# A seven-product form for the third row pair of a decoder's gate and up projection

## The chip, the core and the metric

The kernel runs on one NeuronCore of a Trainium2 chip. The engines named below are TensorE (PE, matrix products; PEld is its loading of the stationary operand), VectorE (DVE), ScalarE (ACT), GpSimd (POOL) and SyncE (SP, which issues most DMAs). They run side by side, each through its own queue of instructions, and wait for one another through semaphores. The metric is the device time of one execution in microseconds, the median of several runs.

## The reference

Two pre-norm residual layers over 256 tokens of width 2048, in float32. Each has a token mixer (HGRN2 in the first, gated linear attention in the second) beside a cross-attention into 256 memory tokens, an output projection, and a SwiGLU feed-forward of inner width 5632. The change lies in the last of these:

```python
hn = _rmsnorm(h, norm_ffn[layer])
gate, up = jnp.split(hn @ w_gate_up[layer], 2, axis=-1)
h = h + (jax.nn.silu(gate) * up) @ w_down[layer]
```

Here `hn` is 256 x 2048 and `w_gate_up[layer]` is 2048 x 11264.

## The kernel before

**Two halves of each number.** Float32 operands are split in two parts of the format fp32r: a high part (a cast on ScalarE) and a low part (the operand minus the high part, on VectorE; once in a block on GpSimd). One product of a 128x128 left block with a 128x512 right block then takes three matmuls: high x high, high x low, low x high. The function `split` (line 276) makes the two parts of a loaded weight tile `raw`; the names `parts148a` to `parts148d` in the trace are those of tile number 148.

**Row pairs.** The 2048 rows of the weight are eight pairs of 256 rows. For one pair and one block of 512 columns of gate and 512 of up, the work is a product of 2 x 2 blocks: two token tiles by two row tiles on the left, two row tiles by two column groups on the right. A plain product has eight block products. A pair of kind **S** does with seven, in Winograd's manner: `seven` (line 420) first splits the weight blocks b00, b11 and b10, then makes three differences and sums on VectorE in place (`raw<-raw`: one of 128x1024, two of 128x512), and splits the results t5, t7, t6, t4. A pair of kind **O** uses eight products and needs no arithmetic on the weights, only on the left factors (`d0`, `d1`). A pair of kind **H** uses eight products too, with one weight difference: one subtraction of 128x512 on VectorE, then the split of the result `e1`. The left factors of each pair are made once a layer by `Forms` (line 359); which there are depends on the pair's letter in `PAIRS` (line 354): six for O (with `d1`, without `s`, `u`, `z`), eight for S, nine for B. A pair whose factors are those of S can be used as S or as H; one with `d1` as O.

**Blocks.** `ffn` (line 1172) runs over 11 blocks of 512 inner columns. `up_block(b)` calls `project_halves` (line 591) with a string of eight letters from `KINDS` (line 1161), one for each pair; blocks from number 4 on use the last string. PE's products of a block accumulate in seven PSUM banks, named `f_p` in the trace. For S the order of the seven products of a pair is 1, 3, 2, 5, 7, 6, 4, and in the block's last pair 1, 2, 6, 7, 5, 4, 3. Then VectorE sums the banks to gate and up (`sums`, the tiles `e` and `s`), ScalarE and VectorE form silu(gate) x up (`gate`), PE transposes the result (`turn`), and two pieces of the down projection of an earlier block follow on PE (`fd` in the trace), each with a copy of `h` into its bank and a give-back to `h` by ScalarE (`h<-fd`).

**Order.** With `Engine.kept` set (line 608, from pair 3 of block 0 on and through all further blocks) the instructions keep the order in which the program names them, on every engine. Small pieces (`sums`, `gate`, `turn`, the give-backs) are put in by keys: `due` files a piece, and `mark` issues all that are due, at places inside the preparation of weights. So what ScalarE and VectorE do between two weight parts is written out by hand.

**Buffers.** `raw` has three buffers. The parts of two row groups (tag `parts`) have six; the parts of a single row group of 512 columns (tag `part`: part a of S, part c of H) have two. A buffer is used again when its readers, matmuls of PE, are done.

The tile numbers in the trace run on: block 0 of layer 0 has 84 to 91, block 1 has 92 to 99, then come tiles of the down projection; block 2 has 102 to 109, block 3 has 112 to 119, block 4 has 124 to 131, block 5 has 136 to 143, block 6 has 148 to 155. Hereafter a pair is named by its place in the block, 0 to 7, or by its tile's number.

Of the kernel before, what the change touches and what calls it, by code (L numbers as in the profile page):

```python
# [26 lines left out]
DFF = 5632  # L27
# [13 lines left out]
def trunk_kernel(ctx: ExitStack, tc: tile.TileContext, x, mem, norm_mix, norm_ffn, norm_mem,  # L41
# [12 lines left out]
    def bank(name):  # L54
        return psum.tile([P, 512], F32, tag="bank", name=name)
# [84 lines left out]
    class Engine:  # L140
        kept = False

        def __init__(self, engine):
            self.engine = engine
            self.last = self.hold = None
# [33 lines left out]
    def mark(key):  # L179
        while waiting and waiting[0][0] <= key:  # L180
            waiting.pop(0)[2]()
# [14 lines left out]
    class Quad:  # L196
# [6 lines left out]
        def x(self, k, t):  # L203
            return self.h[:, k, t * P:(t + 1) * P], self.l[:, k, t * P:(t + 1) * P]
# [13 lines left out]
    def transposes(srcs, name, back=False):  # L218

        ps = aux_ps(name)  # L220
        turns(ps, [src(t) for src in srcs for t in range(NT)], (ident, turned_id if back else ident))
        return ps
# [29 lines left out]
    def later(*pieces):  # L252
        pending.extend(pieces)

    def step():
        if pending:
            piece = pending.pop(0)
            if piece:
                piece()
# [11 lines left out]
    def new_raw():  # L271
        i = n_w[0]
        n_w[0] += 1
        return i, wts.tile([P, 4, 512], F32, tag="raw", name=f"raw{i}", bufs=3)
# [76 lines left out]

    PAIRS = "SSOSSOSB"
    HOMES = (("hq", "hq"),) * 4 + (("F", "K"), ("T", "sc"), ("Q", None), ("v", "gate"))
    FACTORS = {"S": ("x10", "x00", "x01", "x11", "s", "d0", "u", "z"), "O": ("x10", "x00", "x01", "x11", "d0", "d1"),
               "B": ("x10", "x00", "x01", "x11", "s", "d0", "u", "z", "d1")}
# [1 line left out]
    class Forms:  # L359


        def __init__(self, p, name):
            self.kind = PAIRS[p]
            self.names = FACTORS[self.kind]
# [43 lines left out]
    def load_pair(raw, w, p, c0, c1, n):  # L408

        if n_w[0] == 1:  # L410
            for k, j, c in ((0, 0, c0), (0, 1, c1), (1, 3, c0), (1, 2, c1)):
                nc.sync.dma_start(out=raw[:, j, 0:n], in_=w[(2 * p + k) * P:(2 * p + k + 1) * P, c:c + n])
                if k == 0 and c == c1:
                    load_mem(0, 256, 512)
            return
        for j, c in ((slice(0, 4, 3), c0), (slice(1, 3), c1)):
            nc.sync.dma_start(out=raw[:, j, 0:n],
                              in_=w[2 * p * P:(2 * p + 2) * P, c:c + n].rearrange("(k p) c -> p k c", p=P))

    def seven(i, raw, between=None):  # L420

        n = raw.shape[2]
        tt = ve.tensor_tensor
        b00, = split(raw[:, 0:1, :], f"{i}a")
        b11, b10 = split(raw[:, 2:4, :], f"{i}b")
        if between:
            between()

        tt(out=raw[:, 0:2, :], in0=raw[:, 0:4:2, :], in1=raw[:, 1:2, :].broadcast_to([P, 2, n]), op=ALU.subtract)
        tt(out=raw[:, 2, :], in0=raw[:, 2, :], in1=raw[:, 0, :], op=ALU.add)  # L430
        tt(out=raw[:, 3, :], in0=raw[:, 3, :], in1=raw[:, 2, :], op=ALU.subtract)
        t5, t7 = split(raw[:, 0:2, :], f"{i}c")
        t6, t4 = split(raw[:, 2:4, :], f"{i}d")
        return {1: ("x00", b00), 2: ("x01", b10), 3: ("z", b11), 4: ("x11", t4), 5: ("s", t5), 6: ("u", t6), 7: ("d0", t7)}
# [81 lines left out]
    def project_two(pairs, plan, w, c0, c1, n, name, give, view=lambda ps: ps, onto=None, prep=None, behind=None,  # L516
# [10 lines left out]
        else:  # L527
            sevens, plains = iter(range(len(PAIRS))), iter(range(plan.count("S"), len(PAIRS)))
            order = [next(sevens if c == "S" else plains) for c in plan]
# [61 lines left out]
    def project_halves(forms, kinds, w, c0, c1, name, key, keep):  # L591


        left = {b: sum(TIMES[kind][b - 1] for kind in kinds) for b in range(1, 8)}
        ps = {}

        def product(b, left_factor, right):
            first = b not in ps
            if first:
                ps[b] = bank(f"{name}p{b}")  # L600
            left[b] -= 1
            (xh, xl), (hi, lo) = left_factor, right
            pe.matmul(ps[b], xh, hi, start=first, stop=False)
            pe.matmul(ps[b], xh, lo, start=False, stop=False)
            pe.matmul(ps[b], xl, hi, start=False, stop=left[b] == 0)

        for p, kind in enumerate(kinds):
            Engine.kept = keep <= p
            i, raw = new_raw()
            load_pair(raw, w, p, c0, c1, 512)  # L610
            x = forms[p].get
            last = p == len(PAIRS) - 1
            if kind == "S":
                todo = seven(i, raw, lambda: mark(key + p))
                for b in (1, 2, 6, 7, 5, 4, 3) if last else (1, 3, 2, 5, 7, 6, 4):
                    product(b, x(todo[b][0]), todo[b][1])
            else:
                b00, b01 = split(raw[:, 0:2, :], f"{i}a")
                mark(key + p)
                b11, b10 = split(raw[:, 2:4, :], f"{i}b")  # L620
                todo = [[(2, "x00", b00), (5, "x10", b01), (4, "x10", b00), (3, "d0", b01)]]
                if kind == "O":
                    todo.append([(2, "x01", b10), (5, "x11", b11), (4, "x11", b10), (3, "d1", b11)])
                else:
                    ve.tensor_tensor(out=raw[:, 3, :], in0=raw[:, 3, :], in1=raw[:, 2, :], op=ALU.subtract)
                    e1, = split(raw[:, 3:4, :], f"{i}c")
                    todo.append([(2, "x01", b10), (3, "x01", b11), (7, "x11", b11), (4, "x11", e1)])
                todo = [m for ms in zip(*todo) for m in ms] if last else todo[0] + todo[1]
                for b, f, right in todo:
                    product(b, x(f), right)  # L630
            step()
        return ps
# [56 lines left out]
    def more_of(quads, p, tag, name, behind=None):  # L689
        pairs = quads["pairs"]  # L690
        pairs[p] = held(behind, More, quads[p // 2], p % 2, tag, name) if behind else More(quads[p // 2], p % 2, tag, name)

    def quad_pairs(quads):
        quads["pairs"] = {p: Half(quads, p) for p in range(len(PAIRS))}

# [44 lines left out]
    for l in range(2):  # L740
# [6 lines left out]
        if l == 0:  # L747
            later(*[lambda p=p: more_of(memq, p, "hq", f"mem{p}") for p in range(len(PAIRS))
                    if f"{p}S" in MEM[1] and f"{p}S" not in MEM[0]])
# [408 lines left out]
    PARTS = ((0,), (1, 2), (3, 4), (5, 6), (7, 8), (9, 10))  # L1158


    KINDS = ("SHOSHOSO", "HHOSSOSO", "SHOSSOSO", "SSOSSOHS", "SSOSSOSS")

# [7 lines left out]
    def ffn(l, forms, r, after, tail=None):  # L1172
        sq = {}

        def up_block(b):
            ps = project_halves(forms, KINDS[min(b, 4)], w_gate_up[l], 512 * b, DFF + 512 * b, f"f{l}_{b}_",
                                100 * b, 0 if b else 3)
            when = WHEN[min(b, 3)]
            got = {}

            def sums():
                got["e"] = e = work.tile([P, NT, 512], F32, tag="stg", name=f"e{l}_{b}", bufs=2)
                got["s"] = s = work.tile([P, NT, 512], F32, tag="stg", name=f"s{l}_{b}", bufs=2)
                e0, e1, s0, s1 = e[:, 0, :], e[:, 1, :], s[:, 0, :], s[:, 1, :]
                ac.copy(out=e0, in_=ps[1])
                for out, p, q in ((s0, 2, e0), (e1, 6, e0), (s1, 7, e1), (e1, 5, e1), (e0, 5, s1),
                                  (s1, 4, s1), (e1, 3, e1)):
                    ve.tensor_tensor(out=out, in0=ps[p], in1=q, op=ALU.add)
                    if p == 2 and b:
                        free_port.append(ve.last)  # L1190

            def gate():
                e, s = got["e"], got["s"]
                for t in range(NT):
                    ac.activation(out=s[:, t, :], in_=s[:, t, :], func=AF.Silu, scale=r[:, t:t + 1])
                for t in range(NT):
                    ve.scalar_tensor_tensor(out=s[:, t, :], in0=e[:, 1 - t, :], scalar=r[:, t:t + 1], in1=s[:, t, :],
                                            op0=ALU.mult, op1=ALU.mult)

            def turn(j):  # L1200
                if j == 0:
                    sq[b] = Quad("tq", f"s{l}_{b}")
                got[j] = transposes([lambda t, c=(2 * j + i) * P: got["s"][:, t, c:c + P] for i in range(2)],
                                    f"tp_{sq[b].h.name}{j}")

            due(100 * b + when["sums"], sums)
            due(100 * b + when["gate"], gate)
            for j, (k0, k1) in enumerate(when["turn"]):
                due(100 * b + k0, lambda j=j: turn(j))
                due(100 * b + k1, lambda j=j: sq[b].put(2 * j, 2, got[j]))  # L1210
# [178 lines left out]
```

## Time and profile before

| | |
|---|---|
| median of 3 runs | 2271.93 us (2270.59 to 2271.93) |
| the profiled execution, its own time | 2271.69 us |
| its span, first to last instruction | 2269.9 us |
| TensorE clock granted, mean | 0.999 |
| feed-forward of layer 0, blocks 0 to 10, first product to the end of the last `f_p` | 524.2 to 1149.9 us |
| the same of layer 1 | 1572.0 to 2197.9 us |

A block from number 4 on takes 62.30 us in both layers, with one exception of 62.56.

How to read the rows shown below. A timeline row has the start in us from the span's begin, the duration in us, the engine, the line, the operation, what it writes and reads, and in brackets the idle time of the engine before it with what ended that time. Most rows have line 151, that of a helper that records the order, so the tiles' names tell what an instruction is. Where an engine starts an instruction before the end of the one ahead, the step from start to start is what counts. A row of stretches has the length, then busy time (and count) of PE, PEld, DVE, ACT and POOL, the granted clock, the share of the DMA engines and GB/s. One word on blocks: the tile numbers 136 to 143 and the stretch from 838 to 900 us do not belong to the same block; in that stretch PE works on the down projection behind block 5 and then on block 6 (148 to 155).

### The profile page before, as it was taken

Reading aid. Unit: us, or ns where it says so; the run is one execution under the profiler, and the core shown is the slowest. Engines: PE = TensorE matmul, PEld = TensorE weight load, DVE = VectorE, ACT = ScalarE, POOL = GpSimd, SP = SyncE. Lnnn points to the kernel's source line nnn. Section 1 sums busy time; section 2 is a strip of 40 time slices with the busy share of each in tenths; the row PEclk is TensorE's granted clock in tenths of the full one; section 3 lists DMA queues with packets and bytes.
Section 4 is the critical chain, followed back from the end, with each engine's and each line's share of the span. In section 5 each row is a group of like instructions: output and inputs, shape, how many; then the busy total and the mean of one; then the engine's idle time right before and its main releaser. Section 6 shows DMA issues by size and latency. Waiting matters only on the chain.

```text
span 2269.9 us, 29374 instructions
## 1 busy us (share of the span) xinstructions
PE 2250.8 (99%) x10710; PEld 1901.4 (84%) x10710; DVE 2065.8 (91%) x2615; ACT 1423.5 (63%) x1938; POOL 83.4 (4%) x61
## 2 busy tenths in 40 slices
PE   9999999999999999999999999999999999999998
PEld 7888888888888888888889999988888888888887
DVE  7889999899999999999996887899899999999997
ACT  6655656566666666666665665566566666666664
POOL 0000000000000000000000000001000000000000
PEclk9999999999999999999999999999999999999999
DMA  8645545455556665555665446555556565665564
GB/s 289 204 151 183 186 157 177 167 168 203 170 202 222 204 206 190 203 199 204 204 212 174 142 146 190 157 176 203 197 194 203 205 210 194 205 205 202 205 217 153
DMA packets 232644, 435.78 MB, mean 192 GB/s; under 512 B 13199, under 2 KB 42675, under 8 KB 232243
## 3 DMA queue, kind: packets, MB, share of 16 engines
q1 hardware_dynamic: 231203, 429.64, 56.4%
q10 hardware_dynamic: 1296, 4.26, 0.5%
q8 instruction: 84, 1.38, 0.2%
q14 instruction: 61, 0.50, 0.1%
HBM read 430.71 MB, written 3.15 MB: 191 GB/s over the span
## 4 chain that ended last, share of the span: by engine, by line
PE 89%; DVE 6%; ACT 2%; issue 1%; DMA 1%; POOL 0%; SPq 0%; POOLq 0%; DVEq 0%; ACTq 0%
PE f_p L151 39%; PE fd L151 19%; PE wo L151 4%; PE m1p L151 2%; PE wo0p L151 2%; PE hf0p L151 2%; PE wo1p L151 2%; PE fd_0p L151 2%; PE gk1p L151 1%; PE gg11p L151 1%; PE gg10p L151 1%; PE gg01p L151 1%; PE m0p L151 1%; DVE raw L151 1%; PE gx L151 1%
## 5 line engine op out<-in xcount | busy, mean ns | idle before, releaser
L151 DVE TENSOR_TENSOR raw<-raw 128x512 f32<-128x512 f32 (+3 forms) x474 | 403.6, 852 | 9.2
L151 ACT CAST parts<-raw 128x1024 fp32r<-128x1024 f32 (+1 forms) x216 | 212.0, 1016 | 44.6 <-DMA raw<-in_w_down_dram 9.8
L151 DVE TENSOR_TENSOR parts<-raw,parts 128x1024 fp32r<-128x1024 f32 (+1 forms) x196 | 224.0, 1180 | 15.2 <-ACT parts L151 15.1
L286 POOL TENSOR_TENSOR parts<-raw,parts 128x1024 fp32r<-128x1024 f32 x20 | 48.2, 2411 | 1187.1 <-ACT parts L151 1138.6
L151 ACT COPY h<-fd 128x512 f32<-128x512 f32 x80 | 46.3, 588 | 55.0 <-PE fd L151 52.1
L151 ACT ACTIVATE s<-s,rf_r 128x512 f32<-128x512 f32 x44 | 31.8, 722 | 41.6 <-DVE s L151 41.4
L151 DVE TENSOR_TENSOR e<-f_p,e 128x512 f32<-128x512 f32 x66 | 45.2, 685 | 2.3
L151 ACT COPY fd<-h 128x512 f32<-128x512 f32 x82 | 45.2, 582 | 0.0
L151 PE MATMUL fd<-parts,s_6h 128*128 128x512 f32 x128 | 39.8, 392 | 0.0
L151 PE MATMUL fd<-parts,s_8h 128*128 128x512 f32 x128 | 39.8, 392 | 0.0
L151 PE MATMUL fd<-parts,s_4h 128*128 128x512 f32 x128 | 39.8, 392 | 0.0
L151 PE MATMUL fd<-parts,s_2h 128*128 128x512 f32 x128 | 39.8, 392 | 0.0
L151 PE MATMUL fd<-parts,s_0h 128*128 128x512 f32 x128 | 39.8, 392 | 0.0
L151 PE MATMUL fd<-parts,s_5h 128*128 128x512 f32 x128 | 39.4, 389 | 0.0
L151 PE MATMUL fd<-parts,s_3h 128*128 128x512 f32 x128 | 39.4, 389 | 0.0
L151 PE MATMUL fd<-parts,s_7h 128*128 128x512 f32 x128 | 39.4, 389 | 0.0
L151 PE MATMUL fd<-parts,s_1h 128*128 128x512 f32 x128 | 39.4, 389 | 0.0
L151 DVE TENSOR_TENSOR s<-f_p,e 128x512 f32<-128x512 f32 x44 | 30.3, 689 | 4.3 <-PE f_p L151 2.4
L151 DVE SCALAR_TENSOR_TENSOR s<-e,rf_r,s 128x512 f32<-128x512 f32 x44 | 31.0, 747 | 0.2
L151 PEld LDWEIGHTS fd<-parts,s_7h 128*128 128x128 f32 x128 | 24.0, 188 | 5.0
L151 PEld LDWEIGHTS fd<-parts,s_3h 128*128 128x128 f32 x128 | 24.0, 188 | 5.0
L151 PEld LDWEIGHTS fd<-parts,s_1h 128*128 128x128 f32 x128 | 24.0, 188 | 5.0
(5723 smaller groups left out, 7258.1 us busy)
## 6 DMA issues: line engine op xcount, KB each, us to landing
raw<-in_w_gate_up_dram SPq DMA_DIRECT2D x352, 512.0 KB, 3.9
raw<-in_w_down_dram SPq DMA_DIRECT2D x80, 1024.0 KB, 5.7
raw<-in_hgrn_w_in_dram SPq DMA_DIRECT2D x96, 512.0 KB, 3.9
raw<-in_gla_w_in_dram SPq DMA_DIRECT2D x96, 384.0 KB, 3.3
raw<-in_w_out_dram SPq DMA_DIRECT2D x16, 1024.0 KB, 5.8
raw<-in_w_out_dram SPq DMA_DIRECT2D x32, 512.0 KB, 4.1
raw<-in_w_mem_kv_dram SPq DMA_DIRECT2D x30, 512.0 KB, 5.5
raw<-in_w_down_dram SPq DMA_DIRECT2D x16, 512.0 KB, 4.1
```

Source lines behind the costliest of these rows:

```text
L151: ins = func(*args, **kwargs)
L286: low = (nc.gpsimd if free_port else ve).tensor_tensor(out=both[:, 1, k:j, 0:m], in0=src[:, k:j, :], in1=both[:, 0, k:j, 0:m].bitcast(F32) ...
```

## The change

Pair 2 gets the eight left factors of kind S in place of the six of kind O. It can no longer be used as O, since `d1` is missing. So every string of `KINDS` changes in its third letter: in blocks 0 to 3 and in blocks 5, 7 and 9 from O to H, in blocks 4, 6, 8 and 10 from O to S. The same holds in both layers. All other letters stay.

```diff
-    PAIRS = "SSOSSOSB"
+    PAIRS = "SSSSSOSB"
...
-    KINDS = ("SHOSHOSO", "HHOSSOSO", "SHOSSOSO", "SSOSSOHS", "SSOSSOSS")
+    KINDS = ("SHHSHOSO", "HHHSSOSO", "SHHSSOSO", "SSHSSOHS") + ("SSSSSOSS", "SSHSSOSS") * 3 + ("SSSSSOSS",)
...
-            ps = project_halves(forms, KINDS[min(b, 4)], w_gate_up[l], 512 * b, DFF + 512 * b, f"f{l}_{b}_",
+            ps = project_halves(forms, KINDS[min(b, len(KINDS) - 1)], w_gate_up[l], 512 * b, DFF + 512 * b, f"f{l}_{b}_",
```

The number of products that each PSUM bank receives is counted from the string (`left` in `project_halves`, by `TIMES`, line 406), so it follows by itself. The loads of the weights do not change.

## The prediction

> **What bounds the kernel now.** I read the page first: the busy shares, then the chain that ended last.
>
> ```profile
> PE 2250.8 (99%) x10710; PEld 1901.4 (84%) x10710; DVE 2065.8 (91%) x2615; ACT 1423.5 (63%) x1938; POOL 83.4 (4%) x61
> ...
> PE 89%; DVE 6%; ACT 2%; issue 1%; DMA 1%; POOL 0%; SPq 0%; POOLq 0%; DVEq 0%; ACTq 0%
> ```
>
> TensorE looks like the only bound, and fewer matmuls look like the way to gain. But a busy share says nothing of how late the next operand comes, so I took one feed-forward period (block 6 of layer 0 with the down projection ahead of it) and cut it into stages: the time before VectorE's first work on the block's weights, the stretch in which VectorE prepares them, and the rest.
>
> ```profile
> 838.20:850.40 12.20, 12.20 (x55) 10.13 (x54) 10.36 (x13) 8.51 (x13) 2.28 (x1) 1.00 0.81 273
> 850.40:897.20 46.80, 46.80 (x212) 38.58 (x211) 45.71 (x49) 28.30 (x34) 0.00 (x0) 1.00 0.55 185
> 897.20:900.50 3.30, 3.30 (x15) 2.71 (x15) 3.30 (x4) 3.30 (x6) 0.14 (x1) 1.00 0.65 189
> sum 62.30, PE 62.30 PEld 51.42 DVE 59.37 ACT 40.11 POOL 2.42; mean PE 20.77 PEld 17.14 DVE 19.79 ACT 13.37 POOL 0.81
> ```
>
> (Columns: busy of PE, weight loads, DVE, ACT, POOL, then the granted clock.) PE is busy for all 62.30 us. DVE is idle for 2.93 us of the block (62.30 - 59.37), but 1.84 of these lie in the first stage; in the 46.80 us in which it prepares the eight row pairs it is busy for 45.71. So the question is which engine arrives last at the end of that stretch. The timeline of DVE, then of PE:
>
> ```profile
> 895.90 1.23 DVE L151 TENSOR_TENSOR parts155d<-raw,parts155d 128x1024 fp32r<-128x1024 f32 x1
> ```
>
> ```profile
> 896.89 0.78 PE L151 MATMUL f_p<-parts155d,hf_7h 128*128 128x512 f32 x2
> 897.51 0.39 PE L151 MATMUL f_p<-parts155d,hf_7l 128*128 128x512 f32 x1
> ...
> 899.82 0.62 PE L151 MATMUL f_p<-parts155b,hf_7h 128*128 128x512 f32 x2
> 900.27 0.39 PE L151 MATMUL f_p<-parts155b,hf_7l 128*128 128x512 f32 x1
> 900.50 0.62 PE L151 MATMUL fd<-parts,s_3h 128*128 128x512 f32 x2
> ```
>
> The last part of the last pair is done at 897.13 (895.90 + 1.23). The two matmuls that read it first take 0.78 where the same two take 0.62 at 899.82: PE waits 0.16 us for it, and everything behind runs without a gap to the down projection at 900.50, that is 3.37 us after DVE's end. **The up phase of every late block ends 3.37 us after DVE's last part; PE has no slack to give.** Nor can DVE begin sooner:
>
> ```profile
> 850.47 0.69 DVE L151 TENSOR_TENSOR parts148a<-raw,parts148a 128x512 fp32r<-128x512 f32 x1 [1.60 <-ACT parts148a L151]
> ```
>
> ```profile
> 848.66 1.27 ACT L151 COPY h<-fd 128x512 f32<-128x512 f32 x2 [1.78 <-PE fd L151]
> ```
>
> DVE idles 1.60 us before the block's first part, for ScalarE's cast of it; that cast stands in ACT's fixed order behind the give-back of `h`, which waits for the down projection on PE. The start of DVE's chain is thus tied to PE's last block, and its length from 850.47 to 897.13 sets the next end. That 45 us chain is what the change edits.
>
> **The change part by part.** *Matmuls removed.* A pair of kind S makes seven products, O and H eight, of three matmuls each. From 899.82 to 900.50 one product takes 0.68 us, 0.227 a matmul. Eight blocks (numbers 4, 6, 8, 10 in two layers) drop one: 8 x 0.68 = 5.4 us of PE. O to H removes none.
>
> *Pair 2 from O to S* in those eight. Block 6 holds an O (150) beside an S (151), in DVE's order:
>
> ```profile
> 865.50 1.22 DVE L151 TENSOR_TENSOR parts150a<-raw,parts150a 128x1024 fp32r<-128x1024 f32 x1
> 866.64 1.22 DVE L151 TENSOR_TENSOR parts150b<-raw,parts150b 128x1024 fp32r<-128x1024 f32 x1
> 867.77 0.69 DVE L151 TENSOR_TENSOR parts151a<-raw,parts151a 128x512 fp32r<-128x512 f32 x1
> 868.37 1.22 DVE L151 TENSOR_TENSOR parts151b<-raw,parts151b 128x1024 fp32r<-128x1024 f32 x1
> 869.51 2.67 DVE L151 TENSOR_TENSOR raw<-raw 128x1024 f32<-128x1024 f32 x3
> 872.10 1.22 DVE L151 TENSOR_TENSOR parts151c<-raw,parts151c 128x1024 fp32r<-128x1024 f32 x1
> 873.38 1.23 DVE L151 TENSOR_TENSOR parts151d<-raw,parts151d 128x1024 fp32r<-128x1024 f32 x1
> 874.52 0.69 DVE L151 TENSOR_TENSOR parts152a<-raw,parts152a 128x512 fp32r<-128x512 f32 x1
> ```
>
> O costs 867.77 - 865.50 = 2.27 us, S 874.52 - 867.77 = 6.75. The chain grows by **4.48 us** in a block without slack. The saved 0.68 us only makes PE wait longer (4.48 + 0.68 = 5.16 us in all, spread over several pairs). Block: +4.48; eight blocks: 35.8.
>
> *Pair 2 from O to H* in the other fourteen. The one H in a settled block is pair 6 of block 3:
>
> ```profile
> 697.64 1.22 DVE L151 TENSOR_TENSOR parts118a<-raw,parts118a 128x1024 fp32r<-128x1024 f32 x1
> 698.78 1.22 DVE L151 TENSOR_TENSOR parts118b<-raw,parts118b 128x1024 fp32r<-128x1024 f32 x1
> 700.03 0.69 DVE L151 TENSOR_TENSOR raw<-raw 128x512 f32<-128x512 f32 x1
> 701.41 0.69 DVE L151 TENSOR_TENSOR parts118c<-raw,parts118c 128x512 fp32r<-128x512 f32 x1 [0.69 <-ACT parts118c L151]
> 702.02 0.69 DVE L151 TENSOR_TENSOR parts119a<-raw,parts119a 128x512 fp32r<-128x512 f32 x1
> 702.88 1.23 DVE L151 TENSOR_TENSOR parts119b<-raw,parts119b 128x1024 fp32r<-128x1024 f32 x1 [0.18 <-ACT parts119b L151]
> ```
>
> From 118a to 119a pass 4.38 us. The new wait is in it: DVE subtracts, ACT casts the difference, DVE needs the cast (0.69 us idle), and behind that cast stand the next pair's casts on ACT, so 119b comes 0.86 after 119a where 151b comes 0.60 after 151a. H therefore costs 4.38 + 0.26 - 2.27 = **2.37 us** more than O. Blocks 5, 7, 9 have no slack: 6 x 2.37 = 14.2. If something filled the idle time, two instructions of 0.60 would be left: 1.2 each, the low end.
>
> *H in blocks 1, 2, 3.* These have more O and H pairs, so PE has some reserve. An S pair reads the low half of its last part at its 17th matmul, 16 x 0.227 = 3.6 us after its first. The tightest pair of block 3 is 116:
>
> ```profile
> 694.23 1.22 DVE L151 TENSOR_TENSOR parts116d<-raw,parts116d 128x1024 fp32r<-128x1024 f32 x1
> ```
>
> ```profile
> 693.20 0.61 PE L151 MATMUL f_p<-parts116a,hf_4h 128*128 128x512 f32 x2
> ```
>
> It is ready at 695.45, needed at 696.8: reserve 1.4, so H costs 2.37 - 1.4 = 1.0. I take 1.0 for blocks 1 and 2 as well (ends: 0 and 2.37): six blocks, 6.0.
>
> *H in block 0.* No row shows three neighbours of kinds H, H, S. Parts of one 512-column row group have two buffers; with H at pairs 1 and 2 the third such part, 87a, must wait until PE has read 85c, today it needs not.
>
> ```profile
> 528.51 0.62 ACT L151 CAST parts87a<-raw 128x512 fp32r<-128x512 f32 x1
> ```
>
> ```profile
> 534.20 0.62 PE L151 MATMUL f_p<-parts85c,hf_1h 128*128 128x512 f32 x2
> 534.65 0.39 PE L151 MATMUL f_p<-parts85c,hf_1l 128*128 128x512 f32 x1
> ```
>
> ACT's cast then starts at about 535.1, not 528.5. ACT and DVE are in fixed order from pair 3 on, so all casts behind 87a wait. They are 6.6 us late; I take off 0.9, an estimate of how far DVE runs behind ACT at 87a today, so DVE is some 5.7 us late. Part of this goes in idle time at the start of block 1:
>
> ```profile
> 557.78 1.23 DVE L151 TENSOR_TENSOR parts92a<-raw,parts92a 128x1024 fp32r<-128x1024 f32 x1 [1.00 <-ACT parts92a L151]
> 559.83 1.23 DVE L151 TENSOR_TENSOR parts92b<-raw,parts92b 128x1024 fp32r<-128x1024 f32 x1 [0.82 <-ACT parts92b L151]
> ```
>
> 5.7 - 1.82 = 3.9 us reach block 1, whose reserve is already spent: 3.9 a layer, 7.8 (ends: 0, if the wait doesn't arise, and 5.7 a layer).
>
> *At nothing.* The factors of pair 2 are now eight, not six: a few more 128x128 operations like the one below and wider copies, before the blocks begin, an estimate of under 1 us a layer beside PE's `w_out` work; uncovered it would be 2 us in all.
>
> ```profile
> 537.93 0.28 DVE L151 TENSOR_TENSOR hf_7g<-hf_7g 128x128 f32<-128x128 f32 x1
> ```
>
>  SP's issue of the pair's third successor waits for a raw buffer that S holds 4.5 us longer; the load lands in 3.9 us while DVE works through two further pairs (over 4.5 us for even an O and an O):
>
> ```profile
> raw<-in_w_gate_up_dram SPq DMA_DIRECT2D x352, 512.0 KB, 3.9
> ```
>
> **Sum**, against the profiled execution's own 2271.69 us (span 2269.9 and 1.8 around it, 0.24 under the median shown): 35.8 + 14.2 + 6.0 + 7.8 = 63.8, so 2335.5. I say **2335**.
>
> [...]
>
> **The rivals.** *Faster, 2266.* If DVE's lateness were hidden, eight products go: -5.4. One mechanism: DVE runs ahead in the down projection, and the lead lasts through pair 7. It decides if DVE's chain has over 5.2 us of reserve in an S block. Against it: 45.71 of 46.80 busy, and PE's 0.16 us wait. Chance 0.03; no change within the noise 0.02.
>
> *Half hidden, 2297.* DVE could use the whole block's idle time if the 1.60 us before 148a went. Then an S block has 59.37 + 4.48 = 63.85 of DVE work, 1.55 over 62.30, and an H block fits (61.74): 8 x 1.55 + 6.0 + 7.8 = 26. But ACT's order, which makes the 1.60, is not touched. Chance 0.07.
>
> *Clock, 2363.* If PE's new waits lowered its clock, the 15 matmuls behind the last wait of an S block would take 6.8 instead of 3.4 us at half rate: 8 x 3.4 = 27 more. The longest wait of PE on another engine today is 1.5 us, and the granted clock stays 1.00 in the stages quoted:
>
> ```profile
> PE spg L151 <- DVE GQ L151: 1.5, 1, 1.5
> ```
>
> The new waits sum to 5.2 a block but I expect them split over pairs 3, 4 and 7, whose parts are all late. Chance 0.05. [...]
>
> **How the numbers follow.** Forecast 0.83; the rivals as above. Low ends together (1.2 for H in blocks 5, 7, 9; nothing in blocks 0 to 3): 35.8 + 7.2 = 43, 2315. High ends: 35.8 + 14.2 + 14.2 + 11.4 = 76, 2347. I take 2314 to 2347. A measurement here can tell about 0.2% (4.5 us): faster 0.03, same 0.02, slower 0.95.
>
> **What would show it.** Late blocks: period 66.8 us with S and 64.7 with H in place of 62.30, PE waiting on DVE's parts c and d, DVE without idle time but for 148a's and H's. Block 0: ACT's cast of 87a ending a wait on PE at 85c. Wrong if the S blocks shorten, or the wait at a block's first part shrinks.

## The result and the profile after

| | before | after |
|---|---|---|
| median | 2271.8 us (2270.59 to 2271.93, 5 runs) | 2345.15 us (2341.85 to 2349.01, 5 runs) |
| ratio | | 1.0326, 95% interval 1.0314 to 1.0338 |
| span of the profiled execution | 2269.9 us | 2343.5 us |
| mean granted clock | 0.999 | 0.993 |

The change makes the kernel 3.3% slower: 73.6 us of span. The forecast was 2335 us in a range of 2314 to 2347. The page after it, busy shares and chain:

```profile
PE 2273.3 (97%) x10686; PEld 1904.7 (81%) x10686; DVE 2123.9 (91%) x2689; ACT 1446.3 (62%) x1968; POOL 77.7 (3%) x61
...
PE 54%; DVE 30%; issue 7%; ACT 7%; DMA 1%; POOL 0%; ACTq 0%; SPq 0%; DVEq 0%; POOLq 0%
```

PE has 24 matmuls fewer, and its share of the chain fell from 89% to 54%; DVE's rose from 6% to 30%. Busy shares say little of this: DVE stands at 91% in both. Now by stage (busy of PE, PEld, DVE, ACT, POOL, granted clock, DMA): blocks 0 and 1; block 2; block 3; block 5 (H) with the down projection ahead of it; block 6 (S) likewise; then the two 3.4 us stretches at the end of block 6.

```profile
522.55:610.85 88.30, 85.94 (x383) 70.09 (x382) 82.38 (x102) 53.23 (x69) 4.78 (x2) 1.00 0.57 190
610.85:664.62 53.77, 52.87 (x238) 43.57 (x236) 49.62 (x56) 34.29 (x44) 2.94 (x2) 1.00 0.60 201
664.62:717.94 53.32, 52.31 (x235) 43.01 (x233) 51.05 (x56) 34.53 (x44) 0.92 (x2) 1.00 0.56 185
786.28:851.06 64.78, 62.77 (x279) 51.47 (x278) 59.52 (x65) 39.51 (x49) 0.75 (x2) 1.00 0.55 185
851.06:919.40 68.34, 64.50 (x276) 51.89 (x275) 65.07 (x72) 43.13 (x53) 4.04 (x2) 0.98 0.59 194
911.94:915.36 3.42, 1.37 (x5) 0.91 (x6) 3.37 (x4) 3.23 (x4) 0.00 (x0) 1.00 0.06 23
915.36:918.77 3.41, 3.41 (x10) 2.65 (x9) 3.24 (x5) 3.33 (x6) 1.15 (x1) 0.50 0.96 291
```

An H block takes 64.78 us (foretold 64.7) and an S block 68.34 (foretold 66.8), where both took 62.30. The last row has what was thought unlikely: the granted clock is 0.50. The end of that S block on PE, VectorE's last parts, and ScalarE's cast of part d:

```profile
911.43 0.39 PE L151 MATMUL f_p<-parts155b,hf_7l 128*128 128x512 f32 x1
913.23 0.50 PE L151 MATMUL f_p<-parts155d,hf_7h 128*128 128x512 f32 x1 [1.41 <-ACT parts155d L151]
914.49 0.51 PE L151 MATMUL f_p<-parts155d,hf_7h 128*128 128x512 f32 x1 [0.76 <-DVE parts155d L151]
914.83 0.40 PE L151 MATMUL f_p<-parts155d,hf_7l 128*128 128x512 f32 x1
915.07 0.81 PE L151 MATMUL f_p<-parts155c,hf_7h 128*128 128x512 f32 x2
915.67 0.63 PE L151 MATMUL f_p<-parts155c,hf_7l 128*128 128x512 f32 x1
916.10 1.06 PE L151 MATMUL f_p<-parts155c,hf_7h 128*128 128x512 f32 x2
916.96 0.63 PE L151 MATMUL f_p<-parts155c,hf_7l 128*128 128x512 f32 x1
...
919.40 0.40 PE L151 MATMUL fd<-parts,s_3h 128*128 128x512 f32 x1
```

```profile
911.94 1.22 DVE L151 TENSOR_TENSOR parts155c<-raw,parts155c 128x1024 fp32r<-128x1024 f32 x1
913.21 1.23 DVE L151 TENSOR_TENSOR parts155d<-raw,parts155d 128x1024 fp32r<-128x1024 f32 x1
```

```profile
912.13 1.04 ACT L151 CAST parts155d<-raw 128x1024 fp32r<-128x1024 f32 x1 [0.40 <-DVE raw L151]
```

PE waits 1.41 us for ScalarE's half of part d, which had to wait for VectorE's last sum, and 0.76 for VectorE's half. Then matmuls come every 0.43 us (916.10 to 916.96 is two of them), not 0.227. The down projection begins 4.96 us after VectorE's end (914.44), not 3.37: 1.6 us more. That this is the clock is tested below.

### The profile page after: what moved, and what is told of

Same layout as the page of the kernel before. It is cut to its first block, busy times and chain, and to the rows that moved or that the text cites. A ratio compares the mean times of both kernels' runs of the same rounds, so it can differ in the third digit from the quotient of the medians.

```text
span 2343.5 us, 29425 instructions
## 1 busy us (share of the span) xinstructions
PE 2273.3 (97%) x10686; PEld 1904.7 (81%) x10686; DVE 2123.9 (91%) x2689; ACT 1446.3 (62%) x1968; POOL 77.7 (3%) x61
## 4 chain that ended last, share of the span: by engine, by line
PE 54%; DVE 30%; issue 7%; ACT 7%; DMA 1%; POOL 0%; ACTq 0%; SPq 0%; DVEq 0%; POOLq 0%
PE fd L151 14%; DVE raw L151 12%; PE f_p L151 11%; PE wo L151 4%; PE m1p L151 2%; PE wo0p L151 2%; PE wo1p L151 2%; PE fd_0p L151 2%; PE gk1p L151 1%; PE gg11p L151 1%; PE gg10p L151 1%; PE gg01p L151 1%; PE m0p L151 1%; PE gx L151 1%; PE hf0p L151 1%
## 5 line engine op out<-in xcount | busy, mean ns | idle before, releaser
L151 DVE TENSOR_TENSOR raw<-raw 128x512 f32<-128x512 f32 (+2 forms) x512 | 433.7, 848 | 10.3
L151 PEld LDWEIGHTS fd<-parts,s_5h 128*128 128x128 f32 x128 | 24.0, 188 | 5.0
```

Of the source, the lines that this page charges most:

```text
L151: ins = func(*args, **kwargs)
```

## The experiments

In the table, a block's time is the step from its predecessor's end to its own, each end read in PE's timeline as the first `fd` matmul behind the `f_p` run (for blocks 0 and 1 together, from the first `f_p` of the feed-forward). In the last two columns two values are blocks without and with a half-rate stretch (3.4 us at a granted clock of 0.50); every S block of after and e2 holds one. Layers agree within 0.3 us, but for blocks 0 and 1 of e11, where each layer has its value.

| kernel | median us | ratio to before, 95% | 0 and 1 | 2 | 3 | S | H or O, late |
|---|---|---|---|---|---|---|---|
| before | 2271.8 | | 84.95 | 52.57 | 51.89 | | 62.30 (O) |
| after | 2345.15 | 1.0314 to 1.0338 | 88.30 | 53.77 | 53.32 | 68.34 | 64.78 |
| e1 H everywhere | 2318.6 | 1.0197 to 1.0227 | 88.29 | 53.76 | 53.34 | | 64.76, 66.34 |
| e2 S in all late blocks | 2365.84 | 1.0404 to 1.0435 | 88.32 | 53.77 | 53.32 | 68.33 | |
| e3 more matmuls | 2341.38 | 1.0293 to 1.0324 | 88.32 | 53.76 | 53.34 | 66.75 | 64.75, 66.35 |
| e5 no sums | 2315.58 | 1.0181 to 1.0215 | 88.29 | 53.77 | 53.35 | 64.02, 65.62 | 64.77, 66.17 |
| e4 order of last pair | 2316.79 | 1.0184 to 1.0212 | 88.28 | 53.76 | 53.33 | 65.46 | 63.50 |
| e8 difference first | 2337.07 | 1.0278 to 1.0306 | 86.65 | 53.76 | 52.25 | 66.76, 68.33 | 64.78 |
| e11 other ring | 2345.63 | 1.0316 to 1.0347 | 88.95, 88.25 | 53.51 | 53.54 | 66.76, 68.2 | 64.75, 66.10 |
| e12 both H edits | 2317.61 | 1.0193 to 1.0227 | 84.95 | 52.57 | 52.12 | 66.74, 68.32 | 63.59 |
| e13 later give-back | 2336.09 | 1.0277 to 1.0307 | 88.28 | 53.77 | 53.36 | 66.22, 67.78 | 64.78 |
| e10 parts on GpSimd | 2335.29 | 1.0268 to 1.0299 | 86.66 | 53.78 | 52.25 | 66.40 | |
| e14 three edits | 2295.69 | 1.0094 to 1.0128 | 84.95 | 52.57 | 52.14 | 65.47 | 62.34 |
| e7 before, other order | 2267.37 | 0.9977 to 0.9994 | 84.95 | 52.57 | 51.89 | | 62.09 (O) |

The kernel before ran beside each batch: 2270.16 us (e1, e2, e3, e5), 2270.55 (e4, e7, e8, e10), 2269.39 (e11, e12, e13), 2269.72 (e14).

### H alone, and S in every late block

```diff
-    KINDS = ("SHHSHOSO", "HHHSSOSO", "SHHSSOSO", "SSHSSOHS") + ("SSSSSOSS", "SSHSSOSS") * 3 + ("SSSSSOSS",)
+    KINDS = ("SHHSHOSO", "HHHSSOSO", "SHHSSOSO", "SSHSSOHS", "SSHSSOSS")
```

> Pair 2 is H in every block, none is S. Chain theory (VectorE's chain of each late block is tied to the block before and has no slack): every late block 64.7 us instead of 62.30, 14 x 2.45 = 34, and 12 for blocks 0 to 3, so 2317 us; the granted clock stays 1.00, as an H block leaves TensorE busy for nearly half of the window with its longest wait. Rival (only VectorE's total load counts, its lead carries over from block to block): an H block has 61.8 us of VectorE work, fits in 62.30, and the time is about 2284. Rival (H blocks lose to the clock too): over 2325 and half-rate stretches in the clock's record.

```diff
+    KINDS = ("SHHSHOSO", "HHHSSOSO", "SHHSSOSO", "SSHSSOHS", "SSSSSOSS")
```

> Pair 2 is S in all seven late blocks of a layer, H in blocks 0 to 3. Chain theory without the clock: late blocks 66.74 us, 14 x 4.44 + 12 = 74, 2346 us. Chain and clock: each late block has one half-rate stretch of 3.4 us that costs some 1.6 us, 14 of them, late blocks near 68.3 us, so 2368 us. Load theory (VectorE's total): 63.8 us a block, 14 x 1.5 + 12, 2305.

H everywhere took 2318.6 us (2317 expected), though VectorE's work in an H block (60.90 us in a row of e3 below) would fit in 62.30: the lead is not carried from block to block. The clock did not stay at 1.00 as expected: two of the 14 late blocks hold a half-rate stretch (66.34 and 66.15 us). S everywhere took 2365.84 (2368 by chain and clock, 2346 by the chain alone). Two of its blocks, and the half-rate stretch of each:

```profile
849.22:852.64 3.42, 3.42 (x9) 2.69 (x9) 3.31 (x5) 2.87 (x6) 0.57 (x1) 0.50 0.71 235
917.49:920.90 3.41, 3.41 (x9) 2.63 (x9) 3.31 (x5) 2.82 (x5) 0.51 (x1) 0.50 0.69 217
785.49:853.84 68.35, 64.53 (x277) 51.89 (x275) 63.71 (x70) 41.78 (x52) 2.40 (x2) 0.98 0.54 185
853.84:922.17 68.33, 64.54 (x277) 51.85 (x275) 63.73 (x70) 41.82 (x52) 2.42 (x2) 0.98 0.53 184
```

Each of the 14 late blocks holds one. All their starts lie on one grid of 3.413 us, 20 grid steps (68.27 us) apart within a layer. A slowed block takes 68.33 us, 0.06 more than 20 steps, so the next one's waits lie at nearly the same place on the grid, and it holds a half-rate stretch too.

### Is it the clock?

```diff
                     product(b, x(todo[b][0]), todo[b][1])
+                    if last and b == 2 and kinds[2] == "S":
+                        for _ in range(8):
+                            pe.matmul(ps[5], x("x01")[0], todo[2][1][0], start=False, stop=False)
```

> As the changed kernel, with eight further matmuls in the last pair of each S block, in the time in which TensorE waits there (they repeat a product in bank 5, so the output changes). Clock theory: the half-rate stretch comes from too little TensorE work in one window, so with more work it is gone: 2345 - 8 x 1.6 = 2332 us, clock 1.00, though 64 matmuls are added. Rival (the last 1.6 us of an S block are a wait and not the clock): 2345 or, if the matmuls aren't hidden, up to 2345 + 8 x 1.8 = 2360.

The S blocks behave as the clock theory says: with eight more matmuls each they are 1.6 us shorter (66.75 against 68.34) and none holds a half-rate stretch. The sum is a miss: 2341.38 us, not 2332. An S block, an H block, and a later H block:

```profile
718.07:784.85 66.78, 64.49 (x285) 52.20 (x284) 63.65 (x70) 41.72 (x52) 2.35 (x2) 1.00 0.55 189
784.85:849.59 64.74, 62.66 (x279) 51.41 (x278) 60.90 (x67) 40.80 (x51) 2.34 (x2) 1.00 0.56 195
916.33:982.68 66.35, 64.33 (x280) 52.57 (x278) 62.33 (x69) 41.77 (x52) 3.98 (x2) 0.97 0.58 199
```

The third row (clock 0.97) has one: five H blocks hold a half-rate stretch instead. Their waits are no longer than in the kernel after (1.26 and 0.76 us at the end of this block); they now lie within one step of the grid. So I filled the grid of every trace with PE's matmuls (0.227 us for one of 512 columns, narrower ones at their own step from start to start) and set beside it whether the next step ran at half rate (*):

```
after  0.21* 0.21* 0.22* 0.23* 0.28* 0.28* 0.28* 0.29* 0.42  0.43  0.43 ...
e2     0.21* 0.23* 0.24* (nine from 0.25* to 0.27*) 0.27* 0.28* 0.42  0.44 ...
e3     0.24* 0.25* 0.25* 0.27* 0.28* 0.43  0.44  0.45 ...
e5     0.28* 0.28* 0.37* 0.37* 0.38* 0.40 ...
e11    0.24* 0.25* 0.30* 0.31* 0.33* 0.38* 0.38* 0.38  0.41 ...
e12    0.24* 0.26* 0.41* 0.42  0.43 ...
```

Nine traces have half-rate steps ahead of the kernel's end, 56 in all; in these every step filled to less than 0.38 is followed by one, none above 0.41 is. In the other five (before, e4, e7, e10, e14) no step between the first 10 us and the kernel's end is filled to less than 0.42. One of the 56 lies outside the feed-forward, in the mixer of layer 1 (e11, 0.33). In block 6 of the kernel after, the step ahead of the half-rate one (911.95 to 915.36, filled to 0.28) holds two waits, of 1.41 and 0.76 us, not one long one. The two waits of an H block come near:

```profile
843.68:847.09 3.41, 2.02 (x8) 1.13 (x6) 3.29 (x5) 2.79 (x3) 0.00 (x0) 1.00 0.50 195
847.09:850.50 3.41, 2.78 (x12) 2.29 (x13) 3.41 (x5) 3.41 (x6) 0.00 (x0) 1.00 0.42 112
```

Here they are cut by the grid at 847.09, and the clock stays at 1.00.

### Is it VectorE?

```diff
-        tt(out=raw[:, 0:2, :], in0=raw[:, 0:4:2, :], in1=raw[:, 1:2, :].broadcast_to([P, 2, n]), op=ALU.subtract)
-        tt(out=raw[:, 2, :], in0=raw[:, 2, :], in1=raw[:, 0, :], op=ALU.add)
-        tt(out=raw[:, 3, :], in0=raw[:, 3, :], in1=raw[:, 2, :], op=ALU.subtract)
+        if sums:
+            tt(out=raw[:, 0:2, :], in0=raw[:, 0:4:2, :], in1=raw[:, 1:2, :].broadcast_to([P, 2, n]), op=ALU.subtract)
...
-                todo = seven(i, raw, lambda: mark(key + p))
+                todo = seven(i, raw, lambda: mark(key + p), p != 2)
```

> As the changed kernel, but pair 2 of the S blocks leaves out its three sums and differences of weight blocks on VectorE (t5, t6, t7, t4 are then plain weights); ScalarE's casts, the buffers, the loads and TensorE's matmuls stay as they are. Chain theory: VectorE's chain is 2.59 us shorter in eight blocks, TensorE's waits shrink below what halves the clock: 2345 - 8 x (2.59 + 1.6) = 2312 us. Rival (ScalarE's casts or the part buffers set the pace): 2345, unchanged, or at most the clock's 13 us less.

2315.58 us (2312 expected). S blocks without a half-rate stretch fall to 64.02, that is by 2.73 (2.59 expected), with ScalarE's casts and PE's matmuls untouched. Five half-rate steps are left, three in S blocks and two in H blocks, where none was expected.

### What the last pair costs

```diff
-                for b in (1, 2, 6, 7, 5, 4, 3) if last else (1, 3, 2, 5, 7, 6, 4):
+                for b in (1, 2, 7, 5, 6, 4, 3) if last else (1, 3, 2, 5, 7, 6, 4):
```

> As the changed kernel, but the last pair of a block takes its products in the order 1, 2, 7, 5, 6, 4, 3 instead of 1, 2, 6, 7, 5, 4, 3, so that the part that VectorE finishes last (d) is read two products later. Chain theory: the up phase of late blocks ends some 2.0 us after VectorE's last part, not 3.4, and TensorE's idle time is spread so that no window is idle enough to halve the clock: 2345 - 14 x 1.4 - 8 x 1.6 = 2313 us. If the half-rate windows stay: 2326. Rival (the block's end is set by something else, the sums or the buffers): 2345.

> The kernel before with the order 1, 2, 7, 5, 6, 4, 3 in the last pair, nothing else. Chain theory: TensorE waits for the last part for only 0.16 us a late block today, so the gain is at most 16 x 0.16 = 2.6 us, 0.1%: 2269 against 2271.8, hardly to be told from no change. Rival (VectorE's chain is what the time hangs on, all 1.4 us count): 14 x 1.4, 2252.

On the changed kernel 2316.79 us (2313 expected): S and H blocks 1.3 us shorter (1.4 expected), no half-rate step left. On the kernel before 2267.37, ratio 0.9985 (0.9977 to 0.9994): a small gain, but clear of 1. Late blocks take 62.09 us, in which PE is busy throughout and waits for nothing. So the gain is 0.21 us a block, near the 0.16 of wait and not the 1.4, and in the kernel before VectorE's chain set the end of a block by no more than that:

```profile
774.94:837.03 62.09, 62.09 (x279) 51.52 (x278) 59.36 (x65) 40.11 (x50) 2.42 (x1) 1.00 0.59 203
```

### What H costs

```diff
+                if kind == "H":
+                    ve.tensor_tensor(out=raw[:, 1, :], in0=raw[:, 3, :], in1=raw[:, 2, :], op=ALU.subtract)
                 b11, b10 = split(raw[:, 2:4, :], f"{i}b")
...
-                    e1, = split(raw[:, 3:4, :], f"{i}c")
+                    e1, = split(raw[:, 1:2, :], f"{i}c")
```

> As the changed kernel, but a pair of kind H makes its weight difference before the low parts of b11 and b10 and in b01's place, so that ScalarE casts it while VectorE works on. Chain theory: H costs 1.2 us more than O, not 2.45, as its idle time and the late casts behind it go: 6 x 1.25 from blocks 5, 7, 9, and about 5 from blocks 0 to 3, so 2333 us, give or take some 5 as half-rate windows move. Rival (H's price is in the extra instructions and the buffers, not in the wait): 2345.

2337.07 us (2333 expected), but not for the reason given: blocks 5, 7, 9 stayed at 64.78, and the gain is in blocks 0, 1 and 3 (2.7 us a layer) and in one half-rate step fewer. The idle time inside H went, and another came two pairs later. ScalarE, PE and VectorE of this kernel around part a of pair 4 (tile 140):

```profile
821.19 0.62 ACT L151 CAST parts140a<-raw 128x512 fp32r<-128x512 f32 x1 [1.40 <-PE f_p L151]
```

```profile
820.72 0.39 PE L151 MATMUL f_p<-parts138c,hf_2l 128*128 128x512 f32 x1
```

```profile
821.85 0.69 DVE L151 TENSOR_TENSOR parts140a<-raw,parts140a 128x512 fp32r<-128x512 f32 x1 [0.79 <-ACT parts140a L151]
```

The cast starts 0.08 us after the last matmul that reads 138c (820.72 + 0.39): H's difference (`e1` in the code) takes one of the two buffers for parts of one row group, PE reads it last of all, and part a of pair 4 is the second request behind it. In the kernel after the same cast waits too:

```profile
824.15 0.62 ACT L151 CAST parts140a<-raw 128x512 fp32r<-128x512 f32 x1 [0.34 <-PE f_p L151]
```

So H's price may be held from two sides. The next two runs put `e1` in the ring of six in place of the ring of two (`split` takes the ring's tag as an argument), alone and with the edit above:

```diff
-                    e1, = split(raw[:, 3:4, :], f"{i}c")
+                    e1, = split(raw[:, 3:4, :], f"{i}c", tag="parts")
```

> As the changed kernel, but the parts of H's weight difference (e1) lie in the ring of six buffers instead of the ring of two, so that part a of pair 4 need not wait for TensorE's last matmul of pair 2, nor 87a in block 0 for 85c. Two-causes theory (H's 2.45 us is set twice, by VectorE's idle time and by the ring of two, either of which alone gives nearly all): blocks 5, 7, 9 stay near 64.7 us; blocks 0 and 1 lose part of their 3.4 us: 2340 to 2344. Ring-only theory: blocks 5, 7, 9 fall to about 63.5, and the time to 2333.

> As the changed kernel, with both edits of H: the difference made before the low parts, and its parts in the ring of six. Two-causes theory: blocks 5, 7, 9 fall from 64.8 to about 63.5 us, and blocks 0 to 3 lose most of their 6 us a layer: 6 x 1.25 + 2 x 4.5 = 16, so 2329 us, give or take some 4 as half-rate windows move. Rival (a third cause holds H): 64.8 stays.

The ring alone gains nothing (2345.63; late H 64.75, blocks 0 and 1 at 88.95 and 88.25, against what I expected of them). Both together give 2317.61, below the 2329 expected: late H blocks 63.59, blocks 0 to 2 back at the times of the kernel before, and five half-rate steps fewer. Either cause alone keeps the whole price in late blocks (64.78 and 64.75) and most of it in block 2 (53.76 and 53.51). In blocks 0 and 1 the difference first alone gives half of it back, in block 3 three quarters. One late H block with both edits:

```profile
780.58:844.18 63.60, 62.66 (x280) 51.47 (x279) 59.28 (x65) 39.86 (x50) 0.77 (x2) 1.00 0.55 189
```

### Two attempts to make room, and the rest

```diff
-            dict(sums=10, gate=11, turn=((13, 101), (13, 101)), back=(13, 101)))
+            dict(sums=10, gate=11, turn=((13, 101), (13, 101)), back=(100, 101)))
```

> As the changed kernel, but in late blocks the first give-back of h stands behind the first parts of the next block on ScalarE, so VectorE need not idle 1.6 us before them. Chain theory (the chain starts late because of that order): up to 1.6 us a late block, 14 x 1.6 = 22, and fewer half-rate windows: 2310 to 2323 us. Rival (the start is held by the raw buffers, the loads or the PSUM banks): 2345.

2336.09 us, where 2310 to 2323 was expected: S blocks gain 0.5, H none. The wait before 148a became a wait before 149c, as the other give-back stands ahead of that cast. VectorE's row, and ScalarE's:

```profile
873.08 1.23 DVE L151 TENSOR_TENSOR parts149c<-raw,parts149c 128x1024 fp32r<-128x1024 f32 x1 [1.56 <-ACT parts149c L151]
```

```profile
870.83 1.27 ACT L151 COPY h<-fd 128x512 f32<-128x512 f32 x2 [3.63 <-PE fd L151]
872.00 1.05 ACT L151 CAST parts149c<-raw 128x1024 fp32r<-128x1024 f32 x1
```

Next, with e4's and e8's edits and S in all late blocks, the low part of t5 and t7 of pair 2 on GpSimd (`pool` is True for pair 2 alone):

```diff
-        t5, t7 = split(raw[:, 0:2, :], f"{i}c")
+        t5, t7 = split(raw[:, 0:2, :], f"{i}c", 2, pool)
```

> S at pair 2 in all seven late blocks, H in blocks 0 to 3, with both edits above (order of the last pair, difference first), and the low half of t5 and t7 of pair 2 on GpSimd instead of VectorE. Chain theory, if GpSimd's work does not slow VectorE's: the chain grows by 4.44 - 1.28 = 3.2 us in a late block, less 1.5 for the order, 14 x 1.7 = 23, and 7 for blocks 0 to 3: 2302 us, no half-rate windows. If VectorE stands still while GpSimd works (2.4 us): 2336.

2335.29 us, near the 2336 of the second case; S blocks take 66.40, 0.94 more than with the order alone. GpSimd's and VectorE's rows:

```profile
747.35 2.48 POOL L286 TENSOR_TENSOR parts126c<-raw,parts126c 128x1024 fp32r<-128x1024 f32 x1 [29.59 <-ACT parts126c L151]
```

```profile
748.76 2.16 DVE L151 TENSOR_TENSOR parts126d<-raw,parts126d 128x1024 fp32r<-128x1024 f32 x1 [1.19 <-ACT parts126d L151]
```

VectorE has nothing to do in its order until ScalarE's cast of d, 1.19 us later, and then needs 2.16 us for what takes 1.23 when GpSimd rests; all 14 late blocks show this. Against the 1.28 us saved stand 1.19 and 0.93 us lost.

Last, e4's edit with both of H:

> The changed kernel with the order 1, 2, 7, 5, 6, 4, 3 in the last pair and both edits of H. Chain theory, from the parts measured: S blocks 65.5 us as with the order alone, H blocks 62.3 (63.6 less 1.3 for the order), blocks 0 to 3 as before the change, no half-rate windows: 8 x 3.2 = 26, so 2296 us against some 2270: what S costs VectorE remains. Rival (H and the half-rate windows were all that made the change lose): 2266, five below the kernel before.

2295.69 us, where 2296 was expected. Block 4 (S) and block 5 (H):

```profile
712.21:777.67 65.46, 62.87 (x277) 50.71 (x275) 61.91 (x67) 39.45 (x50) 1.19 (x1) 1.00 0.52 178
777.67:840.00 62.33, 62.33 (x279) 51.42 (x278) 60.65 (x67) 40.70 (x52) 2.42 (x1) 1.00 0.59 202
```

H's price is gone but for 0.25 us (62.09 with this order in the kernel before), and so is the clock's. What S costs VectorE's chain is not: 3.4 us over 62.09, where S saves PE 0.68.

## Why the prediction came out as it did

**The bound.** Right. PE had no slack in a late block, and DVE's chain set its end, though by 0.21 us only, as e7 shows. (From 850.47 to 897.13 that chain is 46.7 us long, not 45; no sum uses this.) The rival that the lateness would be hidden (2266) fell with the result; the rival that DVE's total counts (2297) fell with H everywhere, where it asked for 2284 and 2318.6 was measured.

**S for O, 4.48 us.** Right: an S block without a half-rate step takes 66.75 (e3; 66.74 to 66.76 in e8, e11 and e12, which add no matmuls), 4.45 over 62.30; 8 x 4.45 = 35.6 for 35.8. As said, the saved product only lengthened PE's waits.

**H for O, 2.37 us.** Right in size, 2.48 (64.78 - 62.30), 14.9 for 14.2; incomplete in cause. I priced VectorE's idle time and the late casts. The ring of two buffers, which I used for block 0, holds the same price in blocks 5, 7 and 9; only both edits together bring it to 1.29, near the 1.2 that was given as the low end.

**Blocks 0 to 3, 13.8 us.** Blocks 2 and 3 cost 1.20 and 1.43 a layer (1.0 each foretold), blocks 0 and 1 together 3.35 (3.9 + 1.0 foretold): 12.0 for 13.8. ScalarE's cast of 87a did wait for PE to read 85c:

```profile
533.49 0.62 ACT L151 CAST parts87a<-raw 128x512 fp32r<-128x512 f32 x1 [0.80 <-ACT hf_6hl L151]
```

```profile
533.02 0.39 PE L151 MATMUL f_p<-parts85c,hf_1l 128*128 128x512 f32 x1
```

It starts 0.08 us after that matmul's end (533.41), 10.94 us after the feed-forward's first product (522.55) where it was 4.32 before (528.51 - 524.19): the 6.6 foretold. But less of it reached block 1. VectorE's part 94b, before and after:

```profile
575.53 1.22 DVE L151 TENSOR_TENSOR parts94b<-raw,parts94b 128x1024 fp32r<-128x1024 f32 x1
```

```profile
576.14 1.22 DVE L151 TENSOR_TENSOR parts94b<-raw,parts94b 128x1024 fp32r<-128x1024 f32 x1
```

From the first product these are 51.34 and 53.59 us: VectorE is 2.25 us late here, not 3.9. Nor was the ring the only cause of the late cast. In e11, without that wait, it comes right behind that of 86c, 11.06 us after the first product (521.88), and blocks 0 and 1 were as slow:

```profile
532.42 0.61 ACT L151 CAST parts86c<-raw 128x512 fp32r<-128x512 f32 x1
532.94 0.61 ACT L151 CAST parts87a<-raw 128x512 fp32r<-128x512 f32 x1
```

What else holds block 0 there wasn't taken apart further; e12 shows only that both of H's causes together make up all of the 3.35.

**The clock, nothing.** This is the term that was mis-sized. The prediction gave the rival of a lowered clock a chance of 0.05, since the waits would be split, and priced it at 27 us, all 15 matmuls behind the wait at half rate. The waits were split as said; these are PE's in pairs 3 and 4 of block 6:

```profile
890.71 0.50 PE L151 MATMUL f_p<-parts151c,hf_3h 128*128 128x512 f32 x1 [0.28 <-DVE parts151c L151]
896.02 0.50 PE L151 MATMUL f_p<-parts152c,hf_4h 128*128 128x512 f32 x1 [0.46 <-ACT parts152c L151]
897.45 0.50 PE L151 MATMUL f_p<-parts152c,hf_4h 128*128 128x512 f32 x1 [0.93 <-DVE parts152c L151]
```

But the two in pair 7, of 1.41 and 0.76 us, lay in one step of the grid, and in the next the clock was 0.50. (In the kernel before it is 0.50 only from 2265.20 us on, behind PE's last matmul.) The half rate came in all eight S blocks at 1.6 us: 12.7 us. The price was too high: no run shows the half rate over all 15 matmuls behind the wait. In each of the eight blocks the granted clock was 0.50 for one step of 3.413 us, in which at most half, 1.7 us, of PE's work is lost. Without the 12.7 the time would have been 2332.5, some 2.6 under the forecast; the sum of the block terms is 35.6 + 14.9 + 12.0 + 12.7 = 75.2, against 73.6 of span. Most of the rest is in the stages ahead of the feed-forward: in layer 0 it begins 1.6 us earlier (522.55 against 524.19). Of this 0.75 us can be chance, as e7, whose code ahead of it is that of the kernel before, begins at 523.44; no run explains the other half.

That 2345.15 still lies in the range is partly luck. The upper end of 2347 was made of H at its dearest in blocks 0 to 3 (14.2 and 11.4 us), of which 12.0 came; the clock, which the range left out, took up most of what these left free.

The eight half-rate stretches of the kernel after start on one grid of 3.413 us to within 0.003 us, and the step ahead of each is filled to between 0.21 and 0.29. PE's longest wait in its late blocks is 1.41 us.

## What to carry to other kernels

Where, as here, one engine works at 99% and the one that feeds it stands still only at places that are tied to the first, the feeder's chain is the bound too: see how long before its use each operand is ready, and price a change by that chain, not by busy shares. A wait with two causes need not shrink when one is taken away (H blocks took 64.78 and 64.75 us with either gone, 63.59 with both), so before trusting an explanation take the cause away and see whether the time goes. And TensorE's waits can cost more than themselves where they gather: here 1.41 and 0.76 us of them within 3.41 us were followed by 3.41 us at a granted clock of 0.50, 1.6 us more. So read the granted clock of the stretch behind the waits too.

## What the hardware showed that was not expected

- In nine traces TensorE's granted clock was 0.50 for one step of 3.413 us behind every step of the grid that matmuls filled to less than 0.38, and behind none that they filled to more than 0.41 (56 half-rate steps ahead of the kernel's end; between the two values it went both ways by this count).
- The loss repeated where a slowed period came near a whole number of steps: with one S block after another it was 68.33 us (20 steps are 68.27) against 66.75 without a half-rate step; S and H in turn took 133.12 us (39 steps) against 131.5. Whether that is more than a coincidence of lengths no run tells.
- More matmuls made the S blocks of e3 shorter: eight more in each took 1.6 us off (66.75 against 68.34), though five H blocks there held a half-rate stretch instead (66.35 against 64.75).
- A subtraction of 128x1024 on VectorE took 2.16 us instead of 1.23 while GpSimd worked on one of its own, in all 14 late blocks of e10.
